# Softmax scaling, a query's low part and the feed-forward's square as VectorE instructions with other operands, in a block of sparse attention, RWKV-7 and gated delta rule

## The chip, the cores and the metric

One core of a Trainium2 chip runs the whole program. The metric is the device time of one execution in microseconds (us), given as the median of several executions. TensorE (PE; its weight loads are listed as PEld), VectorE (DVE), ScalarE (ACT), GpSimd (POOL) and the DMA queue of SyncE (SP) run beside each other, each through its own list of instructions in a fixed order, and wait for each other on semaphores.

## The reference

A transformer block of 1024 positions and width 1024: a norm and a wide projection, three token mixers, a gated merge, and a feed-forward with squared ReLU. Cut to what the change touches:

```python
def _masked_softmax(s, valid):
    s = jnp.where(valid, s.astype(jnp.float32), NEG)
    p = jax.nn.softmax(s, axis=-1)
    return jnp.where(valid, p, 0.0)
...
    qb = _rms(q.reshape(B, S, G, HG, Dh), q_g)
    gb = jax.nn.sigmoid(gates.astype(jnp.float32))...
    def block(args):                       # 128 queries, 8 heads, 3 branches
        p_c = _masked_softmax(s, cmp_end[None, :] <= t[:, None])           # compressed keys
        p_s = _masked_softmax(s, (kpos <= t[:, None])[:, :, None])         # selected blocks
        p_w = _masked_softmax(s, valid)                                    # window of 512
        o = gg[..., 0:1] * o_c + gg[..., 1:2] * o_s + gg[..., 2:3] * o_w
...
    x = x + merged @ w_out[i]
    h = _rms(x, norm_ffn_g[i])
    x = x + jnp.square(jax.nn.relu(h @ w_ff1[i])) @ w_ff2[i]
```

All 16 blocks of 64 keys are selected here (`NSA_N_SEL = 16`, 1024 positions), so the selected branch is causal attention over all earlier keys.

## The kernel before

Every large matmul is done in three passes with a high and a low part of both operands (`hi`, `lo`). `split` makes them: ACT copies the tile to the high part, and DVE or POOL, by the ratio `div`, subtracts it from the raw tile to give the low part (line 259; `wlo` for weights, `ol` for outputs of a mixer, `fl` for the feed-forward).

The program has stages one after the other: the norm, RWKV, the delta rule, attention, and the tail in two halves of 512 positions. Beside each mixer run "dense" jobs, steps of large matmuls that fill TensorE while the mixer's small steps wait: first the projection (`fill`, tiles `fps`), and from the middle of attention (`end_mixed`) the first half of the tail (merge, output projection, norm, feed-forward). The order on each engine is made at build time: tasks and jobs emit instructions in an order that Python sets, and a list scheduler then reorders them with its own estimates. At run time the order of each engine is fixed.

Attention has 32 units, one for each block of 128 queries and pair of heads. For each head `_nsa_head` computes the scores of three branches: compressed (b = 0, 64 keys), selected (b = 1, 128 to 1024 keys) and window (b = 2, 128 to 640 keys). A branch of over 512 keys is in two pieces, each in one of three PSUM banks (tag "s"). DVE takes each piece's maximum (line 1344); with two pieces line 1347 joins the maxima, ACT takes the exponential with the sum of each row (line 1349), and line 1352 joins the sums. When all three are done, DVE inverts the sums (1355), multiplies them by the three gates `gs` (1356), in the first block by `rowok` (1358), and line 1363 scales the three parts of the tile `P`: the compressed and the window part on POOL (`POOLB = (0, 2)`), the selected part on DVE. `_nsa_pv` then transposes `P` on TensorE in pairs of key blocks into one of two PSUM banks (tag "pt"), copies each pair to a high part `PH` (ACT, 1391) and a low part `PL` (DVE, 1392), and multiplies by the values. Both heads' `P` must be scaled before a unit's transposes.

A query tile of 512 positions and two heads is prepared eight times (`query`, `norm64`): `qrb` broadcasts the norm's factor through TensorE into a bank of tag "pt", DVE multiplies it into `q` (1180), ACT makes four pieces of the high part `QH` (1284) and POOL four pieces of the low part `QL` (1285).

In the feed-forward (`up`), ACT takes the ReLU of the PSUM tile into `fr` (1504) and DVE squares it in place (1505) before it is split.

Of the kernel before, what the change touches and what calls it, by code (L numbers as in the profile page):

```python
# [10 lines left out]
F32 = mybir.dt.float32  # L11
# [3 lines left out]
OP = mybir.AluOpType  # L15
AX = mybir.AxisListType.X
PSUM = bass.MemoryType.PSUM
# [30 lines left out]
FBUF = 2  # L48
OBUF = 4
FBUFS = (5, 6)  # L50
POOLB = (0, 2)
KVBUF = 2
SABUF = 5
AGBUF = 4
# [57 lines left out]
class Block:  # L112
# [1154 lines left out]
    def _nsa_attn(self, K2s, K2w, V2s, V2w, K2c, V2c):  # L1267

        self.mark = mark = [0] * 32 + [9, 9]
        qs = {}  # L1270

        def query(i):
            half, hp = i // 4, i % 4
            nc = self.nc
            q = self.tl("q", 1)
            nc.sync.dma_start(out=q, in_=self.nsa_in[hp, :, half * 512:half * 512 + 512])
            yield NLAT[5]
            QH = self.tl("QH", 2, [P, 2, 512], F32R)
            QL = self.tl("QL", 2, [P, 2, 512], F32R)
            q = yield from self.norm64(q, self.qg, "q")  # L1280
            for e in range(2):
                h = slice(e * 64, e * 64 + 64)
                for x in (e, 1 - e):
                    nc.scalar.copy(QH[x * 64:x * 64 + 64, e], q[h])
                    nc.gpsimd.tensor_tensor(out=QL[x * 64:x * 64 + 64, e], in0=q[h], in1=QH[h, e].bitcast(F32), op=OP.subtract)
            yield NLAT[6]
            qs[i] = QH, QL

        units = []
        for u in range(32):  # L1290
            if u % 4 == 0:
                i = u // 4
                self.task(query(i), u - 5, lambda i=i: i == 0 or ((i - 1) in qs and mark[4 * i - 5] >= 2))
            units.append(self.task(self._nsa_unit(u, qs, (K2s, K2w, K2c), (V2s, V2w, V2c)), u,
                                   lambda u=u: u // 4 in qs and mark[u - 1] >= 1 and mark[u - 2] >= 2))
        self.run(lambda: mark[15] >= 2)
        self.end_mixed()
        self.finish(*units)
# [14 lines left out]
    def _nsa_head(self, qb, g, H, QH, QL, K2s, K2w, K2c):  # L1313
        nc = self.nc
        tt, ts = nc.vector.tensor_tensor, nc.vector.tensor_scalar
        qs = slice(qb % 4 * P, qb % 4 * P + P)
        Pt = self.tl("P", 4, [P, 1728])
# [4 lines left out]
        for lo in range(0, L, 512):  # L1322
            n = min(512, L - lo)
            m = [(n - P, self.mtri)] if lo + n == L else []
            segs[1].append((lo, K2s[:, g, lo:lo + n], n, m))
        for lo in range(W0, W1, 512):
            n = min(512, W1 - lo)
# [6 lines left out]
        mx, sm, mx2, sm2 = st[:, 0], st[:, 1], st[:, 2], st[:, 3]  # L1334
        for b, pieces in enumerate(segs):
# [8 lines left out]
                nc.vector.tensor_reduce(out=(mx if i == 0 else mx2)[:, b:b + 1], in_=ps[:, :n], axis=AX, op=OP.max, negate=True)  # L1344
                tiles.append(ps)
            if len(pieces) == 2:
                tt(out=mx[:, b:b + 1], in0=mx[:, b:b + 1], in1=mx2[:, b:b + 1], op=OP.min)  # L1347
            for i, (c, keys, n, masks) in enumerate(pieces):
                nc.scalar.activation(out=Pt[:, c:c + n], in_=tiles[i][:, :n], func=AF.Exp, bias=mx[:, b:b + 1],  # L1349
                                     accum_out=(sm if i == 0 else sm2)[:, b:b + 1])  # L1350
            if len(pieces) == 2:
                tt(out=sm[:, b:b + 1], in0=sm[:, b:b + 1], in1=sm2[:, b:b + 1], op=OP.add)
            yield NLAT[7]
        r = st[:, 4]
        nc.vector.reciprocal(r, sm)
        tt(out=r, in0=r, in1=self.gs[:, qb, H * 3 + 0:H * 3 + 3], op=OP.mult)  # L1356
        if qb == 0:
            tt(out=r[:, 0:1], in0=r[:, 0:1], in1=self.rowok, op=OP.mult)
        for b in range(3):
            c = segs[b][0][0]  # L1360
            n = sum(x[2] for x in segs[b])
            eng = nc.gpsimd if b in POOLB else nc.vector
            eng.tensor_scalar(out=Pt[:, c:c + n], in0=Pt[:, c:c + n], scalar1=r[:, b:b + 1], scalar2=None, op0=OP.mult)  # L1363
        return Pt

    def _nsa_pv(self, qb, g, hp, Ps, V2s, V2w, V2c):
# [45 lines left out]
    def tail(self, hf, wbufs):  # L1412
# [12 lines left out]
        with pool("tacc") as ap, pool("tw") as wp:  # L1425
# [57 lines left out]
            with pool("th") as hp:  # L1483
# [4 lines left out]
                with pool("tf") as fp:  # L1488
                    G = 4

                    def up(ft):
# [10 lines left out]
                        lo = fp.tile([P, 512], F32R, name="fl", tag="fl", bufs=FBUFS[hf])  # L1502
                        r = fp.tile([P, 512], F32, name="fr", tag="fr", bufs=2)
                        nc.scalar.activation(out=r, in_=ps, func=AF.Relu)
                        tt(out=r, in0=r, in1=r, op=OP.mult)
                        fs.append(self.split(hi, lo, r, FSPLIT))


# [106 lines left out]
```

## Time and profile before

| | us |
|---|---|
| median of 3 runs | 2536.28 (2533.8 to 2540.54) |
| the profiled execution | 2527.64 |
| its span, first to last instruction | 2525.9 |
| TensorE busy in the span | 2377.5 (94%) |
| DVE, ACT, POOL busy | 1472.0, 1043.1, 986.8 |

The profiled execution is one more run of the same program: 1.7 us of it lie outside the span, and it is 8.6 us below the median. Attention runs from about 1170 to 1735 us of the span, the rest of the first half of the tail to 2045, and the second half from there to the end. The granted clock in the tables is that of TensorE as a share of 2.4 GHz, averaged over the stretch. A busy time of matmuls covers overlapping instructions once, so a stretch of TensorE without idle time can still hold slower and faster matmuls.

### The profile page before, as it was taken

The page shows a single profiled execution, that of the slowest core. Times are in us where ns is not written, and L with a number is a line of the kernel's source. Part 1 is how long each engine was busy: PE and PEld are TensorE (multiplying, and loading weights), DVE is VectorE, ACT ScalarE, POOL GpSimd, SP SyncE. Part 2 cuts the span into 40 slices and gives each one's busy share as a digit, 9 for nine tenths or more (in the row PEclk, how much of TensorE's full clock was granted, in tenths as well). Part 3 has the DMA queues.
Part 4 walks back from the last instruction along what each step waited for, and adds up shares of the span by engine and source line. Part 5 has one row for each costly group of instructions (what it writes and reads, how often), then busy time and mean ns, then how long its engine had stood idle before and what let it go on. Part 6 is the DMA issues. An engine that isn't in the chain of part 4 may idle for free.

```text
span 2525.9 us, 37184 instructions
## 1 busy us (share of the span) xinstructions
PE 2377.5 (94%) x13589; PEld 1907.6 (76%) x13589; DVE 1472.0 (58%) x3197; ACT 1043.1 (41%) x2083; POOL 986.8 (39%) x975
## 2 busy tenths in 40 slices
PE   6979899999988999989999999999999998999999
PEld 4757676777776777777887777778888876788887
DVE  4586877663477567232556777766454436545444
ACT  5333433332344433225657665654332334423232
POOL 4444444333322121224545675344333346233232
PEclk9889889999999999989999999999999999999999
DMA  4222222222223122272213331014232354223232
GB/s 137 68 56 65 58 63 58 71 54 74 72 66 83 43 57 73 83 173 80 64 52 114 111 106 57 21 62 128 92 109 84 117 164 157 75 88 111 83 111 92
DMA packets 319718, 216.79 MB, mean 86 GB/s; under 512 B 78486, under 2 KB 273184, under 8 KB 319536
## 3 DMA queue, kind: packets, MB, share of 16 engines
q1 hardware_dynamic: 308672, 195.63, 27.3%
q10 hardware_dynamic: 9792, 17.83, 2.0%
q8 instruction: 107, 1.75, 0.3%
q0 software_dynamic: 1072, 0.96, 0.2%
q14 instruction: 75, 0.61, 0.1%
HBM read 178.16 MB, written 36.22 MB: 85 GB/s over the span
## 4 chain that ended last, share of the span: by engine, by line
PE 72%; DVE 13%; DMA 6%; ACT 4%; issue 2%; POOL 2%; SPq 0%; ACTq 0%; POOLq 0%; DVEq 0%
PE fps L97 53%; PE mps L97 15%; PE mps L101 3%; DVE inv_p L336 2%; DVE inv_u L338 1%; DVE gacc L882 1%; DVE BK L550 1%; DMA cw<-in_nsa_cmp_w_dram 1%; POOL wlo L259 1%; DMA lb<-inv 1%; ACT P L1349 1%; ACT whi L254 1%; DMA wraw<-in_w_branch_dram 1%; DVE ast L1344 1%; DMA gin<-gates 1%
## 5 line engine op out<-in xcount | busy, mean ns | idle before, releaser
L259 POOL TENSOR_TENSOR wlo<-wraw,whi 128x512 fp32r<-128x512 f32 (+2 forms) x408 | 530.0, 1302 | 878.9 <-ACT whi L254 848.5
L254 ACT CAST whi<-wraw 128x512 fp32r<-128x512 f32 (+1 forms) x408 | 286.6, 705 | 632.1 <-PE fps L97 444.8
L97 PE MATMUL fps<-hTh,whi 128*128 128x512 f32 x1024 | 447.3, 439 | 6.5 <-ACT rraw L424 3.5
L97 PE MATMUL fps<-hTh,wlo 128*128 128x512 f32 x1024 | 415.8, 410 | 1.3 <-POOL wlo L259 1.3
L97 PE MATMUL fps<-hTl,whi 128*128 128x512 f32 x1024 | 416.5, 408 | 0.0
L259 DVE TENSOR_TENSOR wlo<-wraw,whi 128x256 fp32r<-128x256 f32 (+1 forms) x207 | 129.7, 629 | 232.5 <-ACT whi L254 227.0
L97 PEld LDWEIGHTS fps<-hTh,whi 128*128 128x128 f32 x1024 | 200.9, 197 | 48.5 <-ACT rraw L424 3.6
L97 PEld LDWEIGHTS fps<-hTh,wlo 128*128 128x128 f32 x1024 | 200.0, 196 | 47.7 <-POOL wlo L259 2.2
L97 PEld LDWEIGHTS fps<-hTl,whi 128*128 128x128 f32 x1024 | 201.8, 197 | 32.3
L97 PE MATMUL fps<-h2h,whi 128*128 128x512 f32 x512 | 200.0, 391 | 1.3 <-DVE h2l L291 1.3
L1363 POOL TENSOR_SCALAR P<-P,ast 128x64 f32<-128x64 f32 (+5 forms) x128 | 137.2, 1088 | 160.0 <-DVE ast L1356 97.1
L97 PE MATMUL fps<-h2l,whi 128*128 128x512 f32 x512 | 199.6, 390 | 0.0
L97 PE MATMUL fps<-h2h,wlo 128*128 128x512 f32 x512 | 199.4, 390 | 0.0
L97 PE MATMUL fps<-whi,fl 128*128 128x512 f32 x512 | 191.0, 389 | 0.0
L97 PE MATMUL fps<-whi,fh 128*128 128x512 f32 x512 | 189.9, 391 | 0.0
L97 PE MATMUL fps<-wlo,fh 128*128 128x512 f32 x512 | 189.0, 389 | 0.0
L1442 DVE TENSOR_TENSOR acc<-fps,acc 128x512 f32<-128x512 f32 x160 | 106.7, 686 | 101.4 <-PE fps L97 101.0
L1349 ACT ACTIVATE P<-mps,ast 128x128 f32<-128x128 f32 (+4 forms) x256 | 124.9, 494 | 75.3 <-DVE ast L1347 45.5
L1344 DVE TENSOR_REDUCE ast<-mps 128x1 f32<-128x128 f32 (+4 forms) x256 | 109.0, 441 | 56.3 <-PE mps L97 53.5
L1392 DVE TENSOR_TENSOR PL<-mps,PH 128x512 fp32r<-128x512 f32 (+2 forms) x168 | 103.3, 619 | 47.7 <-ACT PH L1391 47.0
L1391 ACT CAST PH<-mps 128x512 fp32r<-128x512 f32 (+2 forms) x168 | 88.1, 533 | 63.5 <-PE mps L101 58.1
L97 PEld LDWEIGHTS fps<-h2h,whi 128*128 128x128 f32 x512 | 96.2, 188 | 21.5 <-DVE h2l L291 1.8
(465 smaller groups left out, 4802.0 us busy)
## 6 DMA issues: line engine op xcount, KB each, us to landing
wraw<-in_w_in_dram SPq DMA_DIRECT2D x152, 256.0 KB, 2.9
wraw<-in_w_ff_dram SPq DMA_DIRECT2D x128, 256.0 KB, 2.8
wraw<-in_w_ff_dram SPq DMA_DIRECT2D x64, 512.0 KB, 3.4
gates<-fst ACTq DMA_DIRECT2D x48, 256.0 KB, 2.0
wraw<-in_w_branch_dram SPq DMA_DIRECT2D x48, 256.0 KB, 3.2
gin<-gates SPq DMA_DIRECT2D x48, 256.0 KB, 3.2
wraw<-in_w_out_dram SPq DMA_DIRECT2D x16, 512.0 KB, 3.5
nsa_in<-fst ACTq DMA_DIRECT2D x20, 256.0 KB, 2.1
```

The lines of the kernel that those rows point to most:

```text
L97: return self.note(self.nc.tensor.matmul(out, lhsT=lhsT, rhs=rhs, **kw))
L101: return self.note(self.nc.tensor.transpose(out, x, ident))
L254: nc.scalar.copy(hi, raw)
L259: eng.tensor_tensor(out=lo[:, x], in0=raw[:, x], in1=hi[:, x].bitcast(F32), op=OP.subtract)
L336: nc.vector.tensor_tensor(out=v, in0=lt[:n, s, None, s + 1:].to_broadcast([n, w, w]), in1=u[:n, s + 1:, s + 1:].rearrange("p t c -> p c t" ...
L338: nc.vector.tensor_reduce(out=u[:n, s, s + 1:], in_=v, axis=AX, op=OP.add)
L1344: nc.vector.tensor_reduce(out=(mx if i == 0 else mx2)[:, b:b + 1], in_=ps[:, :n], axis=AX, op=OP.max, negate=True)
L1349: nc.scalar.activation(out=Pt[:, c:c + n], in_=tiles[i][:, :n], func=AF.Exp, bias=mx[:, b:b + 1], accum_out=(sm if i == 0 else sm2)[:, b:b ...
L1363: eng.tensor_scalar(out=Pt[:, c:c + n], in0=Pt[:, c:c + n], scalar1=r[:, b:b + 1], scalar2=None, op0=OP.mult)
L1391: nc.scalar.copy(PH[:n, x0:x1], ps[:n, x0:x1])
L1392: tt(out=PL[:n, x0:x1], in0=ps[:n, x0:x1], in1=PH[:n, x0:x1].bitcast(F32), op=OP.subtract)
L1442: tt(out=acc[:, st, c0:c0 + 512], in0=ps, in1=acc[:, st, c0:c0 + 512], op=OP.add)
```

## The change

The three-column products and the two-operand updates of the softmax become instructions in which the second operand is a per-partition scalar:

- Lines 1347 and 1352 (64 each) become `tensor_scalar` with `mx2` or `sm2` as the scalar; so does 1358.
- Line 1356 (64 of them) is dropped. The gate becomes a second scalar of the scaling of `P`.
- All three scalings of `P` are on DVE: 64 of the compressed part (64 columns) and 64 of the window part (32 of 640 columns, 8 each of 128, 256, 384 and 512) come from POOL.
- The product of line 1180 for queries goes to the PSUM bank of `qrb` in place of the tile `q`, so `QH` and `QL` read PSUM, and the 32 `QL` are on DVE in place of POOL.
- The square of line 1505 takes one factor from PSUM (`ps`) and one from `fr`.

```diff
-POOLB = (0, 2)
...
-            q = yield from self.norm64(q, self.qg, "q")
+            q = yield from self.norm64(q, self.qg, "q", PSUM)
...
                     nc.scalar.copy(QH[x * 64:x * 64 + 64, e], q[h])
-                    nc.gpsimd.tensor_tensor(out=QL[x * 64:x * 64 + 64, e], in0=q[h], in1=QH[h, e].bitcast(F32), op=OP.subtract)
+                    nc.vector.tensor_tensor(out=QL[x * 64:x * 64 + 64, e], in0=q[h], in1=QH[h, e].bitcast(F32), op=OP.subtract)
...
-                tt(out=mx[:, b:b + 1], in0=mx[:, b:b + 1], in1=mx2[:, b:b + 1], op=OP.min)
+                ts(out=mx[:, b:b + 1], in0=mx[:, b:b + 1], scalar1=mx2[:, b:b + 1], scalar2=None, op0=OP.min)
...
-                tt(out=sm[:, b:b + 1], in0=sm[:, b:b + 1], in1=sm2[:, b:b + 1], op=OP.add)
+                ts(out=sm[:, b:b + 1], in0=sm[:, b:b + 1], scalar1=sm2[:, b:b + 1], scalar2=None, op0=OP.add)
...
-        tt(out=r, in0=r, in1=self.gs[:, qb, H * 3 + 0:H * 3 + 3], op=OP.mult)
         if qb == 0:
-            tt(out=r[:, 0:1], in0=r[:, 0:1], in1=self.rowok, op=OP.mult)
+            ts(out=r[:, 0:1], in0=r[:, 0:1], scalar1=self.rowok, scalar2=None, op0=OP.mult)
...
-            eng = nc.gpsimd if b in POOLB else nc.vector
-            eng.tensor_scalar(out=Pt[:, c:c + n], in0=Pt[:, c:c + n], scalar1=r[:, b:b + 1], scalar2=None, op0=OP.mult)
+            ts(out=Pt[:, c:c + n], in0=Pt[:, c:c + n], scalar1=r[:, b:b + 1],
+               scalar2=self.gs[:, qb, H * 3 + b:H * 3 + b + 1], op0=OP.mult, op1=OP.mult)
...
-                        tt(out=r, in0=r, in1=r, op=OP.mult)
+                        tt(out=r, in0=ps, in1=r, op=OP.mult)
```

Line numbers of the changed kernel are one to three lower than those of before from the query on (1180 is 1179, 1285 is 1284, 1344 is 1343, 1347 is 1346, 1363 is 1360, 1392 is 1390).

The change also moves instructions, since the scheduler reorders with the new ones. On DVE, this is the seventh query before, from the product of line 1180 on; `ast` holds the softmax's maxima and sums, `gin` and `ms` belong to the tail's merge:

```order
L1180 SCALAR_TENSOR_TENSOR q<-q,qg,mps 128x512
L1355 RECIPROCAL ast<-ast 128x3
L1356 TENSOR_TENSOR ast<-ast,gs 128x3
L1392 TENSOR_TENSOR PL<-mps,PH 128x512
L1363 TENSOR_SCALAR P<-P,ast 128x768
L1344 TENSOR_REDUCE ast<-mps 128x1 x2
L1347 TENSOR_TENSOR ast<-ast 128x1
L1392 TENSOR_TENSOR PL<-mps,PH 128x512 x2
L1470 SCALAR_TENSOR_TENSOR gin<-gin,fps 128x512
L1392 TENSOR_TENSOR PL<-mps,PH 64x256
L1470 SCALAR_TENSOR_TENSOR gin<-gin,fps 128x512
L1352 TENSOR_TENSOR ast<-ast 128x1
```

and the same query in the changed kernel:

```order
L1179 SCALAR_TENSOR_TENSOR mps<-q,qg,mps 128x512
L1390 TENSOR_TENSOR PL<-mps,PH 128x512
L1343 TENSOR_REDUCE ast<-mps 128x1 x2
L1284 TENSOR_TENSOR QL<-mps,QH 64x512
L1346 TENSOR_SCALAR ast<-ast 128x1
L1468 SCALAR_TENSOR_TENSOR gin<-gin,fps 128x512 x2
L1284 TENSOR_TENSOR QL<-mps,QH 64x512
L1351 TENSOR_SCALAR ast<-ast 128x1
L1343 TENSOR_REDUCE ast<-mps 128x1 x2
L1346 TENSOR_SCALAR ast<-ast 128x1
L1390 TENSOR_TENSOR PL<-mps,PH 128x512
L1284 TENSOR_TENSOR QL<-mps,QH 64x512
```

The four `QL` stand among the maxima and the low parts `PL` (three of them are seen here, the fourth stands nine rows further); `PL`, the maxima and the joins are now spread between them, and the PSUM bank is in use from the first of these rows to the fourth `QL`.

On POOL, these are the first units of attention before; `qrb` is the broadcast for the next query, `wlo` the low part of a weight for the dense matmuls:

```order
L1363 TENSOR_SCALAR P<-P,ast 128x128
L1363 TENSOR_SCALAR P<-P,ast 128x64
L259 TENSOR_TENSOR wlo<-wraw,whi 128x512
L1363 TENSOR_SCALAR P<-P,ast 128x128
L1174 COPY qrb<-r_10709 128x512
L1363 TENSOR_SCALAR P<-P,ast 128x64 x2
L1363 TENSOR_SCALAR P<-P,ast 128x256
L1285 TENSOR_TENSOR QL<-q,QH 64x512 x4
L259 TENSOR_TENSOR wlo<-wraw,whi 128x512
L1363 TENSOR_SCALAR P<-P,ast 128x64
L1363 TENSOR_SCALAR P<-P,ast 128x256
L1363 TENSOR_SCALAR P<-P,ast 128x64
```

and the same place in the changed kernel:

```order
L258 TENSOR_TENSOR wlo<-wraw,whi 128x512
L1173 COPY qrb<-r_10708 128x512
L258 TENSOR_TENSOR wlo<-wraw,whi 128x512 x5
L1173 COPY qrb<-r_11345 128x512
L258 TENSOR_TENSOR wlo<-wraw,whi 128x512
L258 TENSOR_TENSOR ol<-or,oh 128x512
L258 TENSOR_TENSOR wlo<-wraw,whi 128x512 x4
L1173 COPY qrb<-r_11919 128x512
L258 TENSOR_TENSOR ol<-or,oh 128x512
```

The scalings of `P` and the `QL` are gone from POOL, and the splits of weights follow each other directly.

On TensorE the same matmuls are in nearly the same order: the eight broadcasts `qrb` stand within 30 rows of their old places of about 9,400, and attention's last matmul stands in the same row.

## Rows read from the trace of the kernel before

**Rows 1.** The profile's page, engines' busy time, and shares of the chain that ended last.
```profile
PE 2377.5 (94%) x13589; PEld 1907.6 (76%) x13589; DVE 1472.0 (58%) x3197; ACT 1043.1 (41%) x2083; POOL 986.8 (39%) x975
...
PE 72%; DVE 13%; DMA 6%; ACT 4%; issue 2%; POOL 2%; SPq 0%; ACTq 0%; POOLq 0%; DVEq 0%
```

**Rows 2.** Stretches of the span: us, busy us (x) of PE, PEld, DVE, ACT, POOL; clock, DMA.
```profile
1170.00:1735.00 565.00, 544.05 (x3146) 444.96 (x3145) 382.36 (x908) 360.47 (x927) 312.91 (x259) 0.98 0.23 72
...
1410.00:1580.00 170.00, 162.54 (x933) 132.23 (x933) 131.78 (x281) 109.09 (x275) 117.36 (x86) 0.98 0.28 87
...
1735.00:2045.00 310.00, 308.87 (x1367) 255.20 (x1366) 147.09 (x202) 97.24 (x146) 102.91 (x86) 1.00 0.35 114
2045.00:2170.00 125.00, 108.92 (x457) 85.51 (x456) 66.82 (x96) 52.67 (x84) 65.17 (x56) 0.96 0.47 147
2170.00:2526.00 356.00, 350.32 (x1549) 289.33 (x1547) 166.18 (x228) 109.35 (x164) 114.49 (x92) 1.00 0.30 96
```

**Rows 3.** The chain in order of time, a piece of the tail: start, us, what.
```profile
1741.21 291.29 PE fps L97 x1284
```

**Rows 4.** Waits of PE from 1170 to 1735: us in total, times, longest.
```profile
PE mps L97 <- ACT P L1349: 7.0, 11, 1.7
PE mps L97 <- DVE PL L1392: 3.4, 4, 2.1
PE mps L97 <- ACT PH L1391: 3.0, 4, 1.2
```

**Rows 5.** One line's instructions each, whole span: count, shortest/median/longest ns.
```profile
L1347 DVE TENSOR_TENSOR ast<-ast x64: 137/158/2361, 1357.7 to 1718.1; 128x1 f32<-128x1 f32 x64
...
L1352 DVE TENSOR_TENSOR ast<-ast x64: 142/159/1684, 1359.6 to 1719.5; 128x1 f32<-128x1 f32 x64
...
L567 DVE TENSOR_SCALAR n<-n x8: 152/164/687, 111.3 to 536.0; 128x8 f32<-128x8 f32 x8
...
L1505 DVE TENSOR_TENSOR fr<-fr x64: 679/1078/2586, 1654.9 to 2502.7; 128x512 f32<-128x512 f32 x64
```

**Rows 6.** Timelines from 1474 to 1479: start us, us, instruction, idle time before it.
```profile
1475.46 1.22 DVE L1352 TENSOR_TENSOR ast<-ast 128x1 f32<-128x1 f32 x1
...
1475.09 1.57 POOL L259 TENSOR_TENSOR ol<-or,oh 128x512 fp32r<-128x512 f32 x1
...
1477.17 0.69 ACT L1349 ACTIVATE P<-mps,ast 128x512 f32<-128x512 f32 x1 [3.24 <-DVE ast L1347]
...
1478.00 0.50 PE L97 MATMUL mps<-K2s,QH 128*128 128x512 f32 x1 [1.26 <-ACT P L1349]
```

**Rows 7.** DVE from 1170 to 1735 by shape: xcount, busy us, mean ns, idle before.
```profile
L1392 DVE TENSOR_TENSOR PL<-mps,PH 128x512 fp32r<-128x512 f32 x127 | 86.5, 684 | 30.0 <-ACT PH L1391 29.4
...
L1347 DVE TENSOR_TENSOR ast<-ast 128x1 f32<-128x1 f32 x64 | 24.9, 390 | 0.7
L1352 DVE TENSOR_TENSOR ast<-ast 128x1 f32<-128x1 f32 x64 | 19.2, 299 | 31.4 <-ACT P L1349 31.0
L1356 DVE TENSOR_TENSOR ast<-ast,gs 128x3 f32<-128x3 f32 x64 | 18.8, 294 | 1.8
...
L1363 DVE TENSOR_SCALAR P<-P,ast 128x384 f32<-128x384 f32 x8 | 7.0, 870 | 0.2
...
L1363 DVE TENSOR_SCALAR P<-P,ast 128x640 f32<-128x640 f32 x8 | 5.7, 713 | 0.1
...
L1363 DVE TENSOR_SCALAR P<-P,ast 128x512 f32<-128x512 f32 x8 | 4.3, 539 | 0.2
```

**Rows 8.** POOL from 1170 to 1735 by shape.
```profile
L259 POOL TENSOR_TENSOR wlo<-wraw,whi 128x512 fp32r<-128x512 f32 x52 | 66.8, 1287 | 50.5 <-ACT whi L254 50.2
L1363 POOL TENSOR_SCALAR P<-P,ast 128x640 f32<-128x640 f32 x32 | 64.4, 2014 | 0.0
L1285 POOL TENSOR_TENSOR QL<-q,QH 64x512 fp32r<-64x512 f32 x31 | 39.8, 1283 | 5.9 <-ACT QH L1284 4.4
L1363 POOL TENSOR_SCALAR P<-P,ast 128x64 f32<-128x64 f32 x64 | 39.3, 615 | 141.8 <-DVE ast L1356 95.3 <-ACT PH L1391 17.5 <-ACT P L1349 10.7
```

## Prediction

> **What bounds the kernel now.** I read the page first: TensorE is busy for 94% of the span and carries 72% of the chain that ended last; DVE is busy 58%, POOL 39% [rows 1]. So an instruction of DVE or POOL counts only where TensorE waits for it. Next the table of stretches, for where TensorE is not full [rows 2]. In the tail's two long pieces it is busy 308.9 of 310 us and 350.3 of 356 us at full clock, and the chain of the first is one run of 1284 matmuls in 291.29 us [rows 3], 227 ns each, with no gap to close. Between 2045 and 2170 us it is idle for 16 us, at the start of the tail's second half, which the change does not touch. In attention, 1170 to 1735 us, it is busy 544.05 of 565 us: **21 us of idle time**, at a mean granted clock of 0.98, so about 2% of 565 us, **11 us**, goes to stretches at the lower of the two clock levels (1.2 instead of 2.4 GHz). Those 32 us are all that shorter waits can give back as far as these rows show. What TensorE waits for there is the softmax's exponentials, 7.0 us, and the low and high parts of the transposed probabilities, 3.4 and 3.0 us [rows 4].
>
> The next view shows why these are late. The joins of two maxima or two sums move one element per partition, and half of them take no more than 158 or 159 ns, but the longest took 2361 and 1684 ns [rows 5]. A piece of the timeline shows one: at 1475.46 the join of the sums takes 1.22 us while a split of 512 columns runs on POOL from 1475.09 on for 1.57 us; the next maximum waits behind it on DVE, the exponential had waited 3.24 us when it began at 1477.17, and TensorE, which needs its score bank back, 1.26 us [rows 6]. The reader is to see that the instruction did not become larger: it was held until POOL had nearly finished.
>
> **The change part by part, in attention.**
>
> *Joins, 64 and 64.* They cost 24.9 and 19.2 us now; at the median of 0.158 us each they would cost 10.1 and 10.2 us [rows 5, 7]. That is 14.8 + 9.1 = 23.9 us of 44.1 us, 54%, that is only being held. Whether the new form with a scalar operand escapes this, no row of one element shows; the nearest, eight columns of `tensor_scalar`, takes 164 ns at the median but 687 ns at its longest [rows 5]. So between 24 us saved and nothing; I take most of it, 20 us, since seven in eight of that row's kind lie low and POOL will be busy for less time.
>
> *The three-column product.* 64 of them, 18.8 us [rows 7], are gone outright. The ones of line 1358 are 8 and cost nothing.
>
> *Scaling on DVE.* The 64 window parts: 32 of 640 columns at 0.713 us = 22.8 us, and 32 of 128 to 512 columns, no dearer than the 512-column row's 0.539 us, = 17.2 us at most; with the eight-column row as the floor of the small ones, 5 us at least [rows 5, 7]. I take 15. The 64 compressed parts of 64 columns lie between 0.164 and 0.539 us; I take 0.25, close to the smaller row, 16 us. On POOL the 640-column ones took 2.014 us each and the 64-column ones 0.615 us [rows 8]. A second scalar operand has no row; I take it as free, and the range covers it if it isn't.
>
> *Low parts of the query.* 31 on POOL at 1.283 us in this stretch [rows 8]; on DVE a subtraction from PSUM of 512 columns is the `PL` row, 0.684 us [rows 7]: +21.2 us on DVE.
>
> *DVE's sum*: -20 - 18.8 + 22.8 + 15 + 16 + 21.2 = +36 us on 382.4 us, so about 418 of 565 us, 74%; in its fullest piece, 1410 to 1580, it goes from 131.8 of 170 us (78%) to some 84%. *POOL's sum*: it loses 64.4 + 39.3 + 39.8 us by the rows shown and the smaller window parts besides, from 312.9 to under 170 us.
>
> *What TensorE gets from it.* Three rows of waits make 13.4 us [rows 4]. The held part of the joins is 54%, and I take the same share of these waits as theirs: 7.2 us. The lower clock comes after gaps of this kind, and I give back the same share of 11 us: 6.0 us. Against it, DVE's list is 36 us longer in 565 us; spread over all its instructions this makes what queues behind them about 6% later, which on the 7.6 us of idle time that the three rows don't explain and on the rest is about 1 us. Sum: 7.2 + 6.0 - 1 = **12 us less**.
>
> *The feed-forward's square.* 64 of them, 679 ns at best and 1078 ns at the median [rows 5], so some 0.4 us each, 26 us of DVE, would go. Nearly all lie in the tail, where TensorE has no gap [rows 2, 3]: I cost it at nothing. The work that hides it is the next block's matmuls, already in TensorE's list. The PSUM bank is held until DVE has squared instead of until ACT has copied, under 2 us longer; one block of 24 matmuls at 227 ns is 5.4 us, so with two banks in attention the bank is back in time.
>
> The sum is made against the profiled execution, 2527.64 us, which would become 2516. The median of the runs is 8.6 us higher, so I predict a median of **2524 us**.
>
> **A rule weighed against the trace.** The rows show a wide scaling of `P` held like a join: 384 columns take 870 ns on the mean while 512 columns take 539 [rows 7]. The Trainium skill, "SBUF — State Buffer", section "Who interferes with whom", says that VectorE and GpSimd share one pair of ports, that whoever starts first keeps it for the whole instruction, and that a one-input `tensor_scalar` takes the pair too when it runs in a two-port mode, as a subtraction with two SBUF inputs does. By that rule moving `P` to DVE brings 128 more instructions into the contest, and the trace agrees for the 384-column row; it gives the second rival below.
>
> **The rivals.**
>
> *More is given back.* If all idle time of TensorE in attention came from held instructions and POOL's slow scalings, and the lower clock went with it, the gain would be the full 32 us: 2504. Against it: a part of the waits is for ACT itself, whose exponentials and copies stay the same. Chance 0.12.
>
> *The contest only moves.* Now 128 joins lose 23.9 us, 0.19 us each, with POOL busy 312.9 us. After the change 192 scalings and 128 joins can be held, 320 instructions. With POOL at 169 us instead of 313 each would lose 0.19 x 169 / 313 = 0.10 us, 32 us in all: more than the joins lose today. Then the exponentials are as late as before, and DVE's longer list eats what is left: no change within 0.3% (7.6 us, about what this measurement can tell from none), 2529 to 2544. For it: the 687 ns of the eight-column row and the 870 ns above. Against it: the scaling stands at the end of a head, where less waits behind it than behind a join of maxima, in front of which the exponential waits. Chance 0.27.
>
> *The query's bank: slower.* The query's product now stays in one of only two PSUM banks that the transposes of `P` use, until the fourth `QL` is done. In the seventh query that is DVE's list from the product to the last `QL`: the 12 rows shown and 9 more, at least 15 instructions of about 0.68 us (four `QL`, `PL`s, the merge's) and ten small ones, some 12 us, where before the bank came free with the product itself. Meanwhile each pair of key blocks goes through one bank: transpose, `PH`, `PL`, and only then the next. TensorE has about 4.5 us of other work between two pairs there (some 20 matmuls of up to 227 ns), against some 2 us of bare time for one pair, an estimate at `PL`'s 0.684 us for each of the three steps [rows 7]. It decides when ACT's and DVE's queues delay a pair by over 2.5 us; then TensorE waits, in its fixed order. With 7 queries in the stretch and two pairs each, 1.5 us a pair would be 21 us, and with nothing gained 2557. Chance 0.09.
>
> *DVE becomes the bound: slower.* At 84% in the piece from 1410 to 1580 the maxima and `PL` could come late in a row. If TensorE lost 10% of those 170 us, 17 us less the 7 gained is +10, 2546. Against it: its list is in an order that the scheduler made with these instructions in it, and ACT's part of the chain is no longer than before. Chance 0.07.
>
> **How the numbers follow.** The forecast, a gain of 8 to 20 us, has a chance of 0.45; more 0.12; no change 0.27; slower 0.16. Faster by over 0.3% is 0.57, the same 0.27, slower 0.16. For the range I leave out the slowest tenth and the fastest: from 2506, nearly all 32 us, to 2543, where the unchanged case ends. The forecast's own range is 2516 to 2528.
>
> **What the profile after would show.** If right: joins with a longest time well under 1 us and some 21 us in all for both lines; POOL under 170 us in attention; DVE near 418 us there; TensorE's idle time from 21 to about 13 us and a clock of 0.99; the tail's long runs at 227 ns a matmul as before, with the square near 0.69 us and no effect on the span. It is wrong if the joins still reach 1 us or more (the contest only moved), if TensorE waits for transposes of `P` behind `QL` after each `qrb` (the bank), or if maxima and `PL` stand late in DVE's queue with no idle time ahead of them (DVE the bound). What would upset the sum altogether is the new order on all engines: it can open gaps of a microsecond or two that no row of before shows.

## The result, and the profile after

The changed kernel takes 2541.64 us (median of 11 runs, 2539.05 to 2557.59), the kernel before 2530.43 us beside it (11 runs, 2524.19 to 2540.54): ratio **1.0052, 95% interval 1.0033 to 1.0072**. The ratio is that of the means; the two medians give 1.0044. It is slower, by little and clear of the noise; the forecast was 2524 us and faster. The prediction's range, 2506 to 2543 us, reaches this median, but its upper end stood there for the case that nothing changes, counted from 2536 us, and the kernel before ran at 2530 us here. The profiled execution took 2541.05 us with a span of 2539.3 us, 13.4 us more than that of before. In the rows of the changed kernel the exponential is L1348, the join of the sums L1351, and `PH` L1389; `oT` is an output of attention on its way to memory.

The two long runs of the chain that ended last, start, length, and what:

```profile
1755.24 291.29 PE fps L96 x1284
...
2186.37 348.51 PE fps L96 x1536
```

and the second of them in the kernel before:

```profile
2172.74 348.51 PE fps L97 x1536
```

Both are as long as before ([rows 3] has the first), but the first starts 14.0 us later. What is lost is lost ahead of it, and not before attention: up to 1170 us TensorE was busy 1066.10 us, in the kernel before 1065.34 us. The table of stretches (columns as in [rows 2]) shows it:

```profile
1170.00:1735.00 565.00, 532.62 (x3046) 432.86 (x3046) 414.08 (x989) 353.14 (x912) 133.92 (x96) 0.97 0.22 69
1410.00:1580.00 170.00, 154.78 (x870) 125.27 (x869) 129.34 (x277) 102.86 (x255) 68.95 (x48) 0.97 0.27 85
...
1760.00:2045.00 285.00, 285.00 (x1260) 236.00 (x1258) 119.09 (x183) 90.66 (x133) 99.12 (x81) 1.00 0.33 106
```

In these 565 us TensorE is idle for 32.4 us where it was 21.0 [rows 2], and the mean granted clock is 0.97 where it was 0.98 (the prediction expected 13 us and 0.99); VectorE's busy time rose from 382.4 to 414.1 us and GpSimd's fell from 312.9 to 133.9, both about as forecast (418, under 170). The views of single lines show that the edits did what they were to do: the joins are never held any more, and the square and the query's low part have one length.

```profile
L1346 DVE TENSOR_SCALAR ast<-ast x64: 192/204/216, 1353.5 to 1732.5; 128x1 f32<-128x1 f32 x64
...
L1351 DVE TENSOR_SCALAR ast<-ast x64: 195/214/216, 1355.6 to 1733.9; 128x1 f32<-128x1 f32 x64
...
L1503 DVE TENSOR_TENSOR fr<-fps,fr x64: 676/690/694, 1674.6 to 2516.2; 128x512 f32<-128x512 f32 x64
...
L1284 DVE TENSOR_TENSOR QL<-mps,QH x32: 669/688/695, 1164.5 to 1588.0; 64x512 fp32r<-64x512 f32 x32
...
L1360 DVE TENSOR_SCALAR P<-P,ast,gs x192: 268/474/2927, 1173.5 to 1735.3; 128x64 f32<-128x64 f32 x64, 128x640 f32<-128x640 f32 x40, 128x128 f32<-128x128 f32 x16, 128x256 f32<-128x256 f32 x16
```

The last row is where the holding went: one scaling took 2.93 us, while the median is 0.47 us. TensorE's waits from 1170 to 1735 us:

```profile
PE mps L96 <- DVE PL L1390: 7.2, 12, 1.5
PE mps L96 <- ACT P L1348: 6.4, 13, 1.1
PE mps L100 <- DVE PL L1390: 4.3, 7, 1.2
PE mps L96 <- ACT PH L1389: 3.4, 4, 1.5
PE mps L96 <- DVE oT L1400: 3.4, 1, 3.4
PE fps L100 <- DVE h2l L290: 2.2, 3, 1.0
PE mps L100 <- DVE QL L1284: 1.3, 1, 1.3
```

Against [rows 4], the waits for ScalarE's exponentials and `PH` are nearly what they were; those for VectorE's `PL` rose from 3.4 to 11.5 us, and the one for `oT` is 3.4 us where it was 1.0. One case, in the timeline from 1513 to 1523 us (a row with x3 is three instructions, named by the first):

```profile
1513.16 4.53 DVE L1360 TENSOR_SCALAR P<-P,ast,gs 128x64 f32<-128x64 f32 x3
...
1513.32 1.30 POOL L1470 TENSOR_TENSOR ms<-ms,gin 128x512 f32<-128x512 f32 x1 [1.07 <-DVE gin L1468]
...
1514.59 2.75 POOL L258 TENSOR_TENSOR wlo<-wraw,whi 128x1024 fp32r<-128x1024 f32 x1
...
1517.61 0.68 DVE L1475 SCALAR_TENSOR_TENSOR ms<-ms,mh 128x512 fp32r<-128x512 f32 x1
1518.21 1.27 DVE L1343 TENSOR_REDUCE ast<-mps 128x1 f32<-128x512 f32 x2
1519.41 0.57 DVE L1400 TENSOR_TENSOR oT<-mps,otmp 64x128 f32<-64x128 f32 x2
...
1520.13 0.35 PE L96 MATMUL mps<-PH,V2s 128*128 128x256 f32 x1 [3.39 <-DVE oT L1400]
...
1521.96 0.58 PE L96 MATMUL mps<-PL,V2s 128*128 128x256 f32 x1 [1.48 <-DVE PL L1390]
...
1522.06 0.69 ACT L1348 ACTIVATE P<-mps,ast 128x512 f32<-128x512 f32 x1 [5.18 <-DVE ast L1346]
```

Read it by start times. The three scalings of one head (64, 896 and 640 columns: 0.31, 1.73 and 2.66 us) take 4.53 us. The second ends at 1515.11 and the third at 1517.69; GpSimd's sum (1.30 us) ends at 1514.62 and its split (2.75 us) at 1517.34. So each of the two wide ones took until just after a long instruction of GpSimd. A step of the merge, two maxima and `oT` stand behind them in VectorE's order with no idle time ahead; TensorE waits 3.39 us for `oT`, then 1.48 us for `PL`, and ScalarE's next exponential has waited 5.18 us. With little held, the three would take some 1.8 us (0.345 + 0.741 + 0.684, the means in e8 below).

### The profile page after: what moved, and what is told of

Read it like the earlier page. It is cut to its first block, busy times and chain, and to the rows that moved or that the text cites. A ratio compares the mean times of both kernels' runs of the same rounds, so it can differ in the third digit from the quotient of the medians.

```text
span 2539.3 us, 37033 instructions
## 1 busy us (share of the span) xinstructions
PE 2379.9 (94%) x13589; PEld 1907.9 (75%) x13589; DVE 1467.8 (58%) x3293; ACT 1044.7 (41%) x2081; POOL 813.4 (32%) x815
## 4 chain that ended last, share of the span: by engine, by line
PE 43%; DVE 4%; ACT 2%; DMA 2%; issue 1%; POOL 1%; SPq 0%; ACTq 0%; POOLq 0%; DVEq 0%
PE fps L96 36%; PE mps L96 6%; PE mps L100 2%; DVE P L1360 1%; DVE ast L1343 1%; DVE PL L1390 1%; DMA wraw<-in_w_branch_dram 1%; ACT P L1348 1%; POOL wlo L258 1%; DMA gin<-gates 0%; ACT whi L253 0%; DMA wraw<-in_w_out_dram 0%; POOL ms L1470 0%; ACT PH L1389 0%; DMA q<-nsa_in 0%
## 5 line engine op out<-in xcount | busy, mean ns | idle before, releaser
L258 DVE TENSOR_TENSOR wlo<-wraw,whi 128x256 fp32r<-128x256 f32 (+1 forms) x207 | 123.3, 599 | 256.7 <-ACT whi L253 251.1
L1348 ACT ACTIVATE P<-mps,ast 128x128 f32<-128x128 f32 (+4 forms) x256 | 124.6, 492 | 61.3 <-DVE ast L1346 36.4
L1389 ACT CAST PH<-mps 128x512 fp32r<-128x512 f32 (+2 forms) x168 | 88.2, 533 | 78.9 <-PE mps L100 73.6
L96 PEld LDWEIGHTS fps<-h2h,wlo 128*128 128x128 f32 x512 | 96.1, 188 | 20.0
L96 PEld LDWEIGHTS fps<-whi,fl 128*128 128x128 f32 x512 | 96.1, 188 | 19.9
```

The costliest lines, as they stand in the source:

```text
L96: return self.note(self.nc.tensor.matmul(out, lhsT=lhsT, rhs=rhs, **kw))
L258: eng.tensor_tensor(out=lo[:, x], in0=raw[:, x], in1=hi[:, x].bitcast(F32), op=OP.subtract)
L1389: nc.scalar.copy(PH[:n, x0:x1], ps[:n, x0:x1])
```

## The experiments

Each kernel ran in rounds beside the kernel before on its chip; ratios are to that, and differences between ratios of different kernels are worked out from them; such a difference is uncertain by some 0.2 to 0.25% either way. The three columns on the right are of 1170:1735 in one profiled execution, which can lie some 10 us below its kernel's mean (e2, e11): TensorE's idle time is 565 us less its busy time; "held" is what VectorE's instructions take above the lower quartile of their own line and shape, summed over the stretch. The stretch is fixed, so a slower kernel has a little less of its work in it.

| kernel | ratio, 95% interval | TensorE idle, us | VectorE busy, us | held, us |
|---|---|---|---|---|
| before | 1 | 21.0 | 382.4 | 51.5 |
| changed | 1.0052 (1.0033 to 1.0072) | 32.4 | 414.1 | 27.8 |
| e1 joins alone | 0.9965 (0.9952 to 0.9978) | 17.5 | 373.6 | 29.4 |
| e2 scaling alone | 1.0059 (1.0037 to 1.0081) | 32.2 | 415.4 | 57.1 |
| e3 query alone | 1.0026 (1.0013 to 1.0039) | 27.7 | 389.9 | 42.8 |
| e4 order alone | 1.0007 (0.9991 to 1.0024) | 24.6 | 375.9 | 52.7 |
| e5 changed, scaling back | 0.9945 (0.9931 to 0.9958) | 16.5 | 370.3 | 13.5 |
| e6 changed, query back | 1.0052 (1.0037 to 1.0066) | 30.5 | 407.8 | 43.3 |
| e9 e5, compressed part on VectorE | 0.9949 (0.9932 to 0.9966) | 19.2 | 389.1 | 17.4 |
| e10 e5, window part on VectorE | 0.9996 (0.9983 to 1.0009) | 23.5 | 400.3 | 22.2 |
| e11 e5, query back | 0.9978 (0.9963 to 0.9992) | 16.0 | 352.1 | 12.5 |
| e12 e5, both parts on ScalarE | 1.0011 (0.9999 to 1.0022) | 26.7 | 380.9 | 21.7 |
| e7 before, GpSimd's splits out | 0.9965 (0.9953 to 0.9977) | 18.6 | 366.2 | 32.2 |
| e8 changed, GpSimd's splits out | 1.0006 (0.9995 to 1.0017) | 25.0 | 405.8 | 12.1 |
| e15 e5, GpSimd's splits out | 0.9947 (0.9927 to 0.9967) | 16.5 | 369.3 | 9.0 |
| e13 e5, useless work ahead | 0.9970 (0.9953 to 0.9988) | 19.2 | 400.2 | 16.0 |
| e14 the same twice | 0.9986 (0.9967 to 1.0006) | 20.5 | 435.7 | 14.4 |
| e16 e5, useless work in place | 1.0004 (0.9983 to 1.0025) | 26.2 | 406.1 | 15.6 |
| e17 the same twice | 1.0021 (1.0007 to 1.0035) | 33.0 | 442.5 | 12.7 |

**The parts alone (e1 to e4).** The theory was that the scaling of `P` on VectorE makes the loss (A); the rivals that the query's bank and its part on VectorE do (B), or the new order of emission (C). Each of the first three is one part of the change on the kernel before.

e1, the one-column forms: the change's edits of lines 1347, 1352 and 1358, and nothing else.

> The kernel before with one part of the change: the joins of maxima and sums and the mask of the first block take their second operand as a per-partition scalar. Theory A (the loss is the scaling of P on DVE, which POOL's splits now hold up and behind which maxima and low parts queue): this part alone gains, joins near 205 ns with none above 300 ns, TensorE idle in attention 21 us or less, ratio 0.994 to 0.998. Theory B (the loss is the query's PSUM bank and its low parts on DVE): the same. Theory C (the loss is only the new order that the scheduler makes): anywhere from 0.995 to 1.005, with no link to how long the joins are held.

0.9965: the joins take 194 to 217 ns and are worth 0.35%, 9 us.

e2, the scaling:
```diff
-POOLB = (0, 2)
+POOLB = ()
```


> The kernel before with one part of the change: all three scalings of P on DVE, with one scalar, the three-column product kept. Theory A: slower, ratio 1.004 to 1.012, scalings held for up to 3 us, about 20 us of held time more on lines 1347, 1352 and 1363 than a quiet DVE would need, TensorE waits for PL 10 us or more in attention. Theory B: no change or a gain from a quieter POOL, ratio 0.995 to 1.001. Theory C: 0.995 to 1.005.

1.0059 (one execution of six took 6005 us; the ratio leaves it out). Its waits of TensorE:

```profile
PE mps L97 <- ACT P L1349: 10.5, 13, 2.1
PE mps L97 <- ACT PH L1391: 6.3, 6, 2.3
PE mps L101 <- DVE P L1363: 6.2, 4, 2.7
PE mps L97 <- DVE PL L1392: 5.5, 13, 1.1
```

All four are longer than before (7.0, 3.0 and 3.4 us in [rows 4], and 1.4 us for `P`). With a fifth row of 1.3 us the waits for `PL` are 6.8 us, not the 10 expected. The scaling alone loses what the whole change loses.

e3, the query's part: the change's edits of lines 1180 (the product stays in PSUM) and 1285 (`QL` on VectorE).

> The kernel before with one part of the change: the query's product stays in PSUM and its low parts are on DVE. Theory A: little, ratio 0.998 to 1.002. Theory B: slower by most of the change's loss, ratio 1.003 to 1.008, with TensorE's waits for transposes of P right behind each broadcast of a query's norm. Theory C: 0.995 to 1.005.

1.0026: a loss, under half of e2's, above what A expected and short of B.

e4, a control in which only the order of emission differs:
```diff
-NLAT = (1.5, 3.0, 6.0, 0.3, 1.0, 3.0, 6.0, 0.6, 2.0, 0.8)
+NLAT = (1.5, 3.0, 6.0, 0.3, 1.0, 3.0, 6.0, 0.7, 2.0, 0.8)
```


> The kernel before with the same instructions on the same engines in another order: one latency that sets the order in which Python emits attention's steps is 0.7 instead of 0.6. Theories A and B: ratio 0.998 to 1.002, held joins as before. Theory C: as large a difference as the change's, 0.5% to either side.

1.0007, no difference. One other order is no proof for all, but the order alone, by this, is not worth half a per cent.

**Parts undone (e5, e6).** e5 is the changed kernel with the compressed and the window part scaled on GpSimd again:
```diff
+POOLB = (0, 2)
...
-            ts(out=Pt[:, c:c + n], in0=Pt[:, c:c + n], scalar1=r[:, b:b + 1],
-               scalar2=self.gs[:, qb, H * 3 + b:H * 3 + b + 1], op0=OP.mult, op1=OP.mult)
+            eng = nc.gpsimd if b in POOLB else nc.vector
+            eng.tensor_scalar(out=Pt[:, c:c + n], in0=Pt[:, c:c + n], scalar1=r[:, b:b + 1], scalar2=self.gs[:, qb, H * 3 + b:H * 3 + b + 1], op0=OP.mult, op1=OP.mult)
```


> The changed kernel, with the compressed and the window part of P scaled on GpSimd again (still by r and the gate in one instruction). Theory A (the scaling on VectorE is what costs) expects the loss gone: the one-column forms alone gave 0.9965 and the query's part alone 1.0026, together 0.999, so 2526 to 2531 us, ratio 0.997 to 1.0005; VectorE's list some 40 us shorter than in the changed kernel, TensorE's waits for it back under 8 us in 1170:1755. Theory B (the query's bank and its VectorE part) expects 1.003 or more. Theory C (only the order of emission) expects any value within 0.998 to 1.005, with TensorE's waits unlike in kind.

0.9945, 2518.01 us, faster than either kernel and faster than expected. Its chain, its stretch, and its waits of TensorE:

```profile
1736.61 291.29 PE fps L97 x1284
```
```profile
1170.00:1735.00 565.00, 548.53 (x3183) 451.04 (x3182) 370.32 (x882) 363.42 (x933) 226.74 (x229) 0.98 0.23 72
```
```profile
PE mps L97 <- ACT P L1349: 6.5, 6, 1.7
PE mps L101 <- DVE P L1363: 3.2, 2, 2.7
PE mps L97 <- ACT PH L1391: 2.2, 3, 1.3
PE mps L101 <- DVE PL L1392: 1.5, 2, 1.2
...
PE mps L97 <- DVE PL L1392: 0.9, 3, 0.3
```

The waits for `PL` are 2.4 us instead of 11.5, and the long run starts 18.6 us earlier than in the changed kernel. So moving 128 scalings from e5 to VectorE costs 1.0052 - 0.9945 = **1.07%, 27 us**, and all the rest of the change together, with these scalings on GpSimd, gains 0.55%, 14 us.

e5 isn't the kernel before in this part, though. With the gate as a second scalar GpSimd's own scalings are shorter, 88.1 us in this stretch where they were 137.2:

```profile
L1363 POOL TENSOR_SCALAR P<-P,ast,gs 128x640 f32<-128x640 f32 x32 | 28.1, 878 | 0.0
```

The same 32 took 2014 ns each with one scalar [rows 8]. So the price of the move depends on the kernel that it is taken from: 0.59%, 15 us, from the kernel before (e2), and 1.07% from e5. Whether GpSimd's shorter form makes the difference isn't shown; e11 below has it too, and is no faster than e1 without it (0.9978 beside 0.9965).

e6 undoes the query's part (the reverse of e3's diff, on the changed kernel).

> The changed kernel, with the query as before (q in SBUF, its low part on GpSimd). Theory A expects most of the loss left: 0.9965 for the one-column forms and 1.0059 for the scaling, together 1.0024, so 2534 to 2539 us; TensorE still waits 9 us or more for VectorE's PL and oT in 1170:1755. Theory B expects 0.999 or less (2528 us), the loss gone with the bank.

1.0052, as the changed kernel: with the scaling on VectorE the query's part is worth nothing either way. B is out, and the sums of parts do not hold: e3 loses 0.26% on the kernel before.

**Dose (e9, e10), the query once more (e11), ScalarE (e12).** e9 and e10 put one part only on VectorE: in e5's diff `POOLB` is `(2,)` and `(0,)`.

> The changed kernel with only the compressed part of P (64 columns, x64, undisturbed some 0.31 us each, 20 us in all) on VectorE and the window part back on GpSimd: half-way between e5 (0.9945) and the changed kernel (1.0052). Rival A2 (VectorE's longer list) expects a share by undisturbed length, 20 of some 50 us: 0.9945 + 0.004 = 0.9985, 0.997 to 1.000. Rival A1 (held instructions) expects a share by held time, some 6 of 24 us: 0.997 or less.

> The changed kernel with only the window part of P (128 to 640 columns, x64, some 30 us undisturbed) on VectorE and the compressed part back on GpSimd. Rival A2 expects 0.9945 + 0.006 = 1.0005, 0.999 to 1.002; rival A1 0.9945 + 0.008 = 1.0025 or more. If the two parts together cost more than their sum (e9 and e10 both under 0.998), the price sits in VectorE passing a load at which its list no longer drains between two tiles.

The compressed part costs nothing by itself (0.9949 beside 0.9945), the window part 0.51%; both together 1.07%. e9 is where the rival of held instructions had it, e10 where the rival of the longer list had it. So the second one is dear only on top of the first, which neither list length nor held time, taken as a price for each microsecond, gives.

e11 is e5 with the query as before (the reverse of e3's diff).

> The kernel before with the one-column forms, the square and the gate folded into the scaling, which stays on GpSimd; the query as before: e5 without its query part. The query part was worth nothing on top of the scaling (e6 against the changed kernel): then 0.9945, 0.993 to 0.996, the same as e5. If its +0.26% of e3 holds here: 0.992. If it helps where VectorE has room: 0.996 or more.

0.9978: without the query's part e5 loses 0.33%. Its third case came about: the move gains beside the one-column forms and the folded gate (e5 against e11), loses on the kernel before (e3), and does nothing with the scaling on VectorE (e6).

e12 scales both parts on ScalarE, with the gate multiplied into `r` as before (that line and the selected part, which stays on VectorE, aren't shown):
```diff
+            if b in POOLB:
+                nc.scalar.activation(out=Pt[:, c:c + n], in_=Pt[:, c:c + n], func=AF.Copy, scale=r[:, b:b + 1])
```


> The changed kernel with the compressed and the window part of P scaled on ScalarE (by r, which has the gate multiplied in as in the kernel before), neither VectorE nor GpSimd: ScalarE gets 128 instructions more, some 60 to 80 us on 363. VectorE's list and held time as in e5 or less (under 13 us). If the place alone matters (VectorE's list is what is short), 0.995 to 0.998; if ScalarE's exponentials come late behind them, TensorE's waits for ScalarE's P go from 6 us to 12 or more and it is 1.000 to 1.006. I take the second.

1.0011. TensorE's row of waits for the exponentials:

```profile
PE mps L97 <- ACT P L1349: 10.4, 9, 3.0
```

They come later, if less than the 12 us expected; the held time was 21.7 us and not under 13, since the three-column product is back (9.5 us of it).

**Held, or a longer list (e7, e8, e15).** Three kernels without GpSimd's low parts of the merge's weights and inputs in attention, so that little can hold VectorE (`wone` is one constant tile, read in place of each low part; the inputs' low parts likewise, not shown):
```diff
...
+            if self.tasks and one.get("mp"):
+                raw = wp.tile([P, kt, cols], F32, name="wraw", tag="wraw", bufs=TRAW[hf])
+                nc.sync.dma_start(out=raw, in_=src.rearrange("(k p) c -> p k c", p=P))
+                hi = wp.tile([P, kt, cols], F32R, name="whi", tag="whi", bufs=wbufs)
+                nc.scalar.copy(hi, raw)
+                return hi, wone(kt, cols, raw)
```


> The kernel before, without the low parts of the merge's weights and of the merge's inputs as long as attention runs (left out: 75 or so subtractions on GpSimd of 1.3 to 2.5 us; the products read one constant tile instead, so TensorE has the same matmuls). It is one half of a pair with e8 and shows what GpSimd's long instructions cost the kernel before: its compressed and window scaling and its query part stay on GpSimd and still hold VectorE's joins. Expected: 2515 to 2531 us, held time on VectorE 25 to 40 us of the 53 before. Neither theory rests on it alone.

> The changed kernel without the same low parts: GpSimd then has almost nothing left beside attention (about 25 us of sums of the merge and copies), so nothing holds the scaling of P. Rival A1 (the scaling costs because GpSimd's long instructions hold it, up to 2.9 us for one): held time falls from 28 to under 8 us and the kernel is at or below e7, ratio to e7 0.995 to 1.000. Rival A2 (the scaling costs because VectorE's list is longer by its undisturbed length, 40 us or so, and maxima and PL stand behind it): it stays slower than e7 by 0.3 to 0.6%, 8 to 15 us, with TensorE's waits for VectorE's PL and oT still 7 us or more in attention.

> e5 without the low parts of the merge's weights and inputs as long as attention runs (left out as in e7 and e8, so that GpSimd holds little): the partner of e8, from which it differs only in the place of the compressed and the window scaling. If held instructions make most of the 1.08% between e5 and the changed kernel, e8 (1.0006) is within 0.4% of it: 0.997 or more. If the list alone makes it, the whole 1.08% stands between them: 0.990. Half and half would be 0.9945.

The stretch 1170:1735 of e15, and of e8 with its scalings by shape, now with little held:

```profile
1170.00:1735.00 565.00, 548.50 (x3199) 449.88 (x3198) 369.30 (x885) 365.09 (x939) 161.49 (x186) 0.99 0.24 74
```
```profile
1170.00:1735.00 565.00, 540.03 (x3133) 439.34 (x3132) 405.76 (x1002) 358.21 (x925) 71.78 (x55) 0.99 0.23 71
```
```profile
L1360 DVE TENSOR_SCALAR P<-P,ast,gs 128x640 f32<-128x640 f32 x40 | 26.7, 684 | 0.0
L1360 DVE TENSOR_SCALAR P<-P,ast,gs 128x64 f32<-128x64 f32 x64 | 22.0, 345 | 1.6
...
L1360 DVE TENSOR_SCALAR P<-P,ast,gs 128x896 f32<-128x896 f32 x8 | 5.9, 741 | 0.0
```

With held time at 12.1 us (under 8 expected), e8 stays 0.41% above e7, as the rival of the longer list has it; its waits for `PL` and `oT` are 6.7 us, where that rival expected 7 or more. e15 is the cleaner partner, for it differs from e8 in the place of the scaling alone: 1.0006 - 0.9947 = **0.59%, about half and half** of the 1.07%, so neither cause alone.

**Length by itself (e13, e14, e16, e17).** e13 adds useless maxima to e5 at the compressed and the window part, e14 twice as many:
```diff
+            if b in POOLB:
...
+                src = self.ident[:, None, :].to_broadcast([P, k, P]) if k else self.ident[:, None, :64]
+                for _ in range(1):
+                    nc.vector.tensor_reduce(out=junk[:, :max(k, 1)], in_=src, axis=AX, op=OP.max)
```


> e5 (the scaling of the compressed and the window part on GpSimd, 0.9945) with useless work on VectorE where the changed kernel scales: at each of the 128 places one maximum over a constant tile, of about the length of the scaling undisturbed (0.22 us for 64 columns, 0.28 to 0.7 us for the window), 45 to 50 us in all over the program, written to a tile that nobody reads and in a form that e5 does not hold. Rival A2 (the length of VectorE's list) expects what e8 shows without held instructions: 1.001 to 1.005. Rival A1 (held instructions, or P itself coming late) expects 0.9945 to 0.997.

> e13 with the useless maximum twice, 90 to 100 us in all. Rival A2 expects a rise that steepens, since VectorE then passes 80% of 1170:1735: 1.010 or more. Rival A1 expects 0.995 to 0.999.

Inconclusive: nothing tied the maxima to their head, and the scheduler put them ahead of it, as the first and last start of the line show.

```profile
L1367 DVE TENSOR_REDUCE junk<-ident x128: 168/244/689, 1148.8 to 1256.4; 128x1 f32<-128x64 f32 x64, 128x4 f32<-128x512 f32 x32, 128x1 f32<-128x128 f32 x16, 128x2 f32<-128x256 f32 x8
```

e16 and e17 tie each to the factor of its head:
```diff
+                    nc.vector.tensor_reduce(out=junk, in_=r[:, b:b + 1].to_broadcast([P, k]), axis=AX, op=OP.max)
```


> The test that e13 was meant to be. The useless maxima of e13 read a constant and were all issued ahead of the attention (1148 to 1256 us); here each reads the factor r of its own P, so that it stands where the changed kernel scales (128 of them, sized for 0.3 us at the compressed part and 0.35 to 0.6 us at the window, 50 to 60 us in all), and P itself is scaled on GpSimd as in e5 (0.9945 to 0.995). Rival A2 (list length) expects what e8 against e15 shows, +0.6%: 1.000 to 1.002. Rival A1 expects 0.9945 to 0.9965; then the 0.6% of e8 against e15 would come from P being scaled late in VectorE's order, not from its length.

> e16 with each maximum twice, 100 to 120 us in all: VectorE's undisturbed work then is well above the changed kernel's, with little held. If the length of the list makes the loss, 1.008 or more, slower than the changed kernel; if not, 0.995 to 0.999.

The line of these maxima in e16, and TensorE's waits there from 1170 to 1735 us:

```profile
L1366 DVE TENSOR_REDUCE junk<-ast x128: 267/330/617, 1182.3 to 1730.3; 128x1 f32<-128x160 f32 x64, 128x1 f32<-128x448 f32 x32, 128x1 f32<-128x192 f32 x8, 128x1 f32<-128x256 f32 x8
```
```profile
PE mps L97 <- ACT P L1349: 8.6, 11, 1.8
PE mps L97 <- DVE PL L1397: 5.0, 9, 1.0
PE mps L101 <- DVE PL L1397: 4.1, 5, 1.9
```

With VectorE busy 406.1 us as in e8, held time as in e5, and `P` itself scaled on GpSimd, e16 takes 1.0004: 0.59% above e5, the same as e8 above e15. TensorE waits 9.1 us for `PL`, where e5 has 2.4 and the changed kernel 11.5. So length alone, at that place, costs these 0.59%. e17 is 1.0021, less than the 1.008 expected: the second dose costs 0.17% where the first cost 0.59%, each uncertain by 0.25%.

## Why the prediction was wrong

The gain came about, in part by luck. The joins alone give 0.35%, 9 us (e1), and the change without the moved scalings 0.55%, 14 us (e5); the sum's gain was 7.2 + 6.0 us. The joins did about as their term said: 13.1 + 13.5 us after, where the text had 20 us less than 44.1. Their new form is never held, but costs 46 to 55 ns more than the old one undisturbed. But 0.33% of e5's gain goes with the query's part (against e11), to which the sum gave nothing, and the second term, 6.0 us given back by the clock, isn't seen: in the one profiled execution of e5 the granted clock is 0.98, as before, and in the changed kernel 0.97. By the prediction's own reckoning, 3% in place of 2% of 565 us, the changed kernel loses some 6 us there. (What it calls 11 us at the lower level is the time lost; at half speed that is some 23 us spent at it.)

**The step that failed is the last of the sum**, "Against it, DVE's list is 36 us longer ... about 1 us". Most of that added work is the moved scalings, and moving them measured 27 us against e5, and 15 us on the kernel before (e2). The list's length was forecast well (414 us for 418). What was wrong is its price. I spread 36 us evenly over 565 and charged 6% of the idle time not yet explained. But the instructions are not spread: up to three stand in a row at the end of each head, and the next head's maxima, the `PL`s and `oT` behind them are what ScalarE and TensorE wait for. An engine busy for 73% is no bound, and its queue is still late where it matters.

Of the 27 us, about 15 (0.59%, some 6 us either way) are the length of the list at that place: e16, where nothing of `P` moves and little is held, and e8 against e15, where little is held, give it independently. The other 12 us (0.48%, some 8 us either way) go with GpSimd's long instructions: this is the part that is gone when they are taken away (1.07% less 0.59%), and the timeline at 1513 shows a mechanism for it. No run adds holding by itself, so this half is a difference; that holding makes it is argued and not shown.

By its other steps:

- *The contest only moves* (0.27) had a mechanism that the rows show, with too low an end. It forecast 32 us of new holding; 23.8 us of the 27.8 held in the changed kernel are in the scalings. Its "against it", that less waits behind a scaling, is what the timeline at 1513 speaks against. It ended at no change because it set holding against holding and left the length out. The rule that gave it, the Trainium skill's "SBUF — State Buffer", "Who interferes with whom", is borne out for the wide scalings by the 4.53 us above; the joins' one-column form shows nothing of it (not held in 128 instructions).
- *DVE becomes the bound* (0.07) had the right sign and nearly the size, 10 us slower, and its sign, maxima and `PL` late with no idle time ahead of them, is what the timeline shows; its place, 1410 to 1580, holds 7.8 of the 11.4 us of new idle time. VectorE there is busy 129.3 of 170 us, 76% and not 84%: late, and not full.
- *The query's bank* (0.09) is refuted: TensorE waited once for `QL`, 1.3 us, and e6 is the changed kernel's time.
- *The square* at nothing: the long runs are 291.29 and 348.51 us in the changed kernel, as before. No run has the square alone.
- *The moved scalings' own length* was low: 64 columns take 0.345 us with little held (e8) and 0.404 in the changed kernel (25.9 us in all; 0.25 and 16 were put down), 640 columns 0.684 and 0.822 (0.713 put down).
- *A new order that opens gaps* was named as what would upset the sum; e4, the one other order tried, moved nothing measurable.

Open: why the same move costs 0.59% on the kernel before (e2), 0.74% between e11 and e6, and 1.07% between e5 and the changed kernel; why the compressed part, 20 us, is free by itself and costs 0.56% behind the window part; and whether e17's second dose really costs less than e16's. The three prices of the move differ by little more than their intervals. By e9 and e10 the price per microsecond of VectorE's list is not constant, and these runs do not say what sets it.

The version to keep is e5 (or e9, the same within the intervals): the one-column forms, the folded gate, the square from PSUM and the query's low part on VectorE, with the scaling left on GpSimd: 2518 us, 0.55% under the kernel before and 1.07% under the changed one.

## What to carry to other kernels

Price work that is moved to an engine by what stands behind it in that engine's order, not by the engine's share of busy time: 36 us of added busy time at the ends of the heads (370 to 406 us, e5 and e16) cost some 15 us on an engine that was then busy for 72% of the stretch. When instructions are held by a neighbour, moving the neighbour's work over can bring wider instructions into the same contest; changing only the form of the small ones (e1) gave its gain without that. Time the parts of a bundle each alone and each undone: here one part hid a gain of 14 us that the others had, and the parts did not add.

## What the runs showed that was not expected

- A `tensor_scalar` of one element in each partition, with a scalar from memory, was not held once in 128 (at most 216 ns) beside GpSimd's long instructions, and again not in e1 (at most 217 ns), while some of the wider ones were, from 64 columns (2.2 us) to 1024 (2927 ns).
- GpSimd's scaling of 640 columns takes 878 ns with two scalars (e5) and 2014 ns with one (the kernel before); the second scalar makes the instruction shorter there. No run tells why.
- On VectorE a second scalar makes it longer. Of the 512-column scalings one in 16 was held in the changed kernel (1511 ns); they average 600 ns with two scalars, and 539 without the held one:

```profile
L1360 DVE TENSOR_SCALAR P<-P,ast,gs 128x512 f32<-128x512 f32 x16 | 8.9, 600 | 0.0
```

  With one scalar, in e2, they average 545 ns, and 479 without the held one (1530 ns). So the second, which the prediction took as free, costs some 55 to 60 ns:

```profile
L1363 DVE TENSOR_SCALAR P<-P,ast 128x512 f32<-128x512 f32 x16 | 8.1, 545 | 0.0
```
